# A two-layer hybrid trunk: the mixers' order on four engines laid out by a planner in the source, small transfers on SP's queue

## The chip, the cores and the metric

The kernel runs on one core of one Trainium2 chip. Its engines are TensorE (PE), VectorE (DVE), ScalarE (ACT), GpSimd (POOL) and SyncE (SP), whose queue issues most transfers. Each engine carries out its own instructions in the order in which they stand, and semaphores hold an instruction until what it needs is there. The metric is the time of one execution on the device in microseconds.

## What is computed

528 positions (16 learned meta tokens and 512 inputs) of width 1024 pass through two layers. Each layer has a mixer and a feed-forward block:

```python
def mixer_sublayer(h, ...):
    u = rms_norm(h, pre_g)
    z = jnp.einsum("bld,de->ble", u, w_in)
    q, k, v, f_logit, a_val, a_gate, sc_b, sc_c, sc_x = jnp.split(z, idx, axis=-1)
    log_f = jax.nn.log_sigmoid((f_logit + b_forget).astype(jnp.float32))
    y_attn = forgetting_attention(q.reshape(hs), k.reshape(hs), v.reshape(hs), log_f)   # 8 heads of 64
    a = a_val * jax.nn.sigmoid(a_gate)
    a = causal_depthwise_conv(a, a_dw_w) + a_dw_b                                       # 31 taps, 256 columns
    a = jax.nn.silu(layer_norm(a, a_ln_g, a_ln_b))
    y_conv = jnp.einsum("blc,ce->ble", a, a_pw_w)
    y_sc = sc_b * causal_depthwise_conv(sc_c * sc_x, sc_conv_w)                         # 3 taps, 256 columns
    y = jnp.concatenate([y_attn, y_conv, y_sc], axis=-1)
    y = jnp.einsum("ble,ed->bld", head_rms_norm(y, head_g), w_out)
    return h + rms_norm(y, post_g)

def ffn_sublayer(h, ...):
    z = causal_depthwise_conv(jnp.einsum("bld,df->blf", rms_norm(h, pre_g), w_up), conv_w)
    g, up = jnp.split(z, 2, axis=-1)
    return h + rms_norm(jnp.einsum("blf,fd->bld", jax.nn.silu(g) * up, w_down), post_g)
```

The attention's logits are q.k / 8 + F[t] - F[s] under a causal mask, with F the running sum of log_f.

## The kernel before

Everything is laid out with features on the 128 partitions and positions along the free axis, in two halves of 264 positions. Each float32 factor of a product is split into a high and a low part of a type that TensorE takes at one pass, and a product is three matmuls, high x high, low x high and high x low (`mm3`, L250). A weight chunk is 128 x 1024 (eight blocks of 128 x 128): SP loads it (`raw`, three buffers, L230), ScalarE rounds it (`whi`, L234) and VectorE subtracts (`wlo`, L235); `whi` and `wlo` have three buffers as well. A projection of one chunk is 24 matmuls of 264 columns for each half.

A mixer (`mixer`, L398) does this:

- `first` (L268): the gate and value of the conformer branch and sc_c and sc_x of the first two groups, the first half ahead of the mixer, the second half in it (L464 to L467). `gated` (L454) makes sigmoid times value out of them.
- `proj` (L411): one chunk, both halves; q, k, sc_b, sc_c, sc_x use it. `v_proj` (L610) has two chunks with the positions on the output's partitions, and 8 columns more for the forget gate (`forget_gate`, L633).
- `conv_taps` (L528): 31 taps for each of two groups, one VectorE instruction of 528 columns each; `conv_tail` (L536): layer norm, SiLU, the pointwise product and the head norms.
- `head_max` (L699): for one head, six logit matmuls (`s`), a masked maximum on VectorE (L713), its diagonal on GpSimd (L717) and one matmul that spreads it (L722). `head_exp` (L727): six blocks of keys; for each two logit matmuls (`st`, L746), exponential on ScalarE (L748), a cut on GpSimd where the block is on the diagonal (L751), rounding on ScalarE (L758), subtraction on VectorE (L759), and three matmuls with v (`acc`, L762). `att_norm` (L769): the head norm of a pair, with float32 matmuls (L777).
- `q_proj` and `k_proj` copy q and k once more by transfers (L683, L695), and `gate_rows` (L664) writes two rows of F beside each head's k (L668), for heads 4 to 7 by way of memory (`g_dram`). ScalarE's queue issues all of these.

`mixer_steps` (L110) is a list of such steps by hand, and the program is written down in its order. Which instruction stands where on an engine is then decided by the framework's scheduler, by its own estimates; only the norms' parts ahead and the output stages (`finish`, L792) have TensorE's order fixed by `manual_schedule`. PSUM has eight banks: in a mixer three `mm`, two `s1`, two `st` and one `acc` (L471 to L478, L737). After a mixer, `finish` multiplies the eight y tiles by w_out, beginning with y0, y1, y2, y4, y5, y6, then y7 and at last y3, and the feed-forward block follows.

Of the kernel before, what the change touches and what calls it, by code (L numbers as in the profile page):

```python
# [9 lines left out]
F32 = mybir.dt.float32  # L10
F32R = mybir.dt.float32r
# [25 lines left out]
NEG = -1e30  # L37

# [71 lines left out]
def mixer_steps():  # L110


    return [("sc_c", 0), ("sc_x", 0), ("sc_b", 0), ("q", 0), ("k", 0), ("v", 0), ("max", 0),
            ("q", 1), ("max", 1), ("k", 1), ("exp", 0), ("sc_norm", 0), ("max", 2), ("exp", 1), ("max", 3), ("norm", 0),
            ("v", 1), ("exp", 2), ("q", 2), ("exp", 3), ("k", 2), ("norm", 1), ("max", 4),
            ("q", 3), ("max", 5), ("exp", 4), ("k", 3), ("exp", 5), ("max", 6), ("norm", 2), ("sc_c", 1), ("max", 7),
            ("exp", 6), ("sc_x", 1), ("pw", 0), ("exp", 7), ("sc_b", 1), ("norm", 3), ("sc_norm", 1)]
# [3 lines left out]
def tile_hybrid_trunk(ctx: ExitStack, tc: tile.TileContext, xT, wflat, pv_d, out):  # L121
# [13 lines left out]
    PE = mybir.EngineType.PE  # L135
# [109 lines left out]
    def next_w():  # L245
        prefetch(1 + AHEAD)
        return ready.popleft()[1]

# [19 lines left out]
    class First:  # L268
# [3 lines left out]
        def __init__(self, rhs, n, groups):  # L272
            self.rhs, self.n, self.groups = rhs, n, groups
            self.ws, self.ps = {}, {}

        def group(self, hf, g, hooks=None):

            items = self.groups[hf][g]
            for i in items:
                if i not in self.ws:  # L280
                    self.ws[i] = next_w()
# [12 lines left out]

# [103 lines left out]
    def mixer(l, ypool, first, close_first):  # L398
# [11 lines left out]

        def proj():  # L411

            w = next_w()
            out = []
            for hf in range(2):
                d = half()[:, :H]
                mm3({hf: d}, w, range(KD), u_rhs)
                out.append((lambda t, hf=hf: t[:, half_sl(hf)], d))
            return out

        def ytiles(i):
            return (T(ypool, [P, L], F32R, f"yhi{i}"), T(ypool, [P, L], F32R, f"ylo{i}"))

        def head_norm(i, yt, hs, eps):

            yhi, ylo = ytiles(i)
            for hf in range(2):
                c = half_sl(hf)
                r = rsqrt2(mp, hs[hf], eps, H)
                nc.vector.scalar_tensor_tensor(yt[:, c], in0=yt[:, c], scalar=gcol("head_g", i), in1=r,  # L430
                                               op0=ALU.mult, op1=ALU.mult)
                nc.scalar.copy(yhi[:, c], yt[:, c])
                nc.vector.tensor_sub(ylo[:, c], yt[:, c], yhi[:, c].bitcast(F32))
            y[i] = (yhi, ylo)

        def plain_head_norm(i, yt, sq):
            hs = []
            for hf in range(2):
                nc.scalar.activation(sq[:, half_sl(hf)], yt[:, half_sl(hf)], AF.Square)
                ps = half()  # L440
                nc.tensor.matmul(ps[:, :H], lhsT=bd, rhs=sq[:, half_sl(hf)], start=True, stop=True)
                hs.append(ps[:, :H])
            head_norm(i, yt, hs, RMS_EPS)
# [3 lines left out]
        for j in range(2):  # L447
# [4 lines left out]
            conv.append(T(mp, [P, L], F32, "cacc", 2))  # L452

        def gated(hf, j):  # L454
            c = half_sl(hf)
            sig = sigs[j][:, c]
            nc.scalar.activation(sig, first.ps[hf, 2 * j], AF.Exp, scale=-1.0)
            nc.scalar.activation(sig, sig, AF.Ln, bias=c_one)
            nc.scalar.activation(sig, sig, AF.Exp, scale=-1.0)
            nc.vector.tensor_mul(apads[j][:, CK - 1 + H * hf:CK - 1 + H * (hf + 1)], first.ps[hf, 2 * j + 1], sig)  # L460

        for j in range(2):
            gated(0, j)
        for j in range(2):  # L464
            first.group(1, j)
            gated(1, j)
        first.group(1, 2)  # L467
# [3 lines left out]
        def half():  # L471
            return T(pp, [P, 512], F32, "mm", 3)

        def s1_tile():
            return T(pp, [P, 512], F32, "s1")

        def st_tile():
            return T(pp, [P, 512], F32, "st")  # L478

        ap = ms.enter_context(tc.tile_pool(name=f"ap{l}", bufs=1, side="right", reuse_waits="tile"))  # L480
# [8 lines left out]
        causal = T(ap, [P, 400], F32, "causal")  # L489
# [38 lines left out]
        def conv_taps():  # L528
            for j in range(2):
                nc.vector.tensor_scalar(conv[j], in0=apads[j][:, :L], scalar1=col("a_dw_w", CK * j),  # L530
                                        scalar2=col("a_dw_b", j), op0=ALU.mult, op1=ALU.add)
                for i in range(1, CK):
                    nc.vector.scalar_tensor_tensor(conv[j], in0=apads[j][:, i:i + L], in1=conv[j],  # L533
                                                   scalar=col("a_dw_w", CK * j + i), op0=ALU.mult, op1=ALU.add)

        def conv_tail():  # L536

            w = next_w()
            a2 = [ytiles(4), ytiles(5)]
            sq = [T(mp, [P, L + CK - 1], F32, "apad", 2) for _ in range(2)]  # L540
            for hf in range(2):
                c = half_sl(hf)
                ps = half()
                for j in range(2):
                    nc.tensor.matmul(ps[:, :H], lhsT=om_c, rhs=conv[j][:, c], start=j == 0, stop=j == 1)
                for j in range(2):
                    nc.vector.tensor_sub(conv[j][:, c], conv[j][:, c], ps[:, :H])
                    nc.scalar.activation(sq[j][:, c], conv[j][:, c], AF.Square)
                ps2 = half()
                for j in range(2):  # L550
                    nc.tensor.matmul(ps2[:, :H], lhsT=om_c, rhs=sq[j][:, c], start=j == 0, stop=j == 1)
                r = rsqrt2(mp, ps2[:, :H], LN_EPS, H)
                for j in range(2):
                    n = conv[j][:, c]
                    nc.vector.scalar_tensor_tensor(n, in0=n, scalar=gcol("a_ln_g", j), in1=r,
                                                   op0=ALU.mult, op1=ALU.mult)
                    nc.vector.tensor_scalar(n, in0=n, scalar1=col("a_ln_b", j), scalar2=None, op0=ALU.add)
                    s = sq[j][:, c]
                    nc.scalar.activation(s, n, AF.Exp, scale=-1.0)
                    nc.scalar.activation(s, s, AF.Ln, bias=c_one)  # L560
                    nc.scalar.activation(s, s, AF.Exp, scale=-1.0)
                    nc.vector.tensor_mul(n, n, s)
                    nc.scalar.copy(a2[j][0][:, c], n)
                    nc.vector.tensor_sub(a2[j][1][:, c], n, a2[j][0][:, c].bitcast(F32))
            yts = []
            for m in range(2):
                yt = T(mp, [P, L], F32, "cacc", 2)
                for hf in range(2):
                    ps = half()
                    mm3({hf: ps[:, :H]}, w, range(2), lambda b, k, hf: a2[k][b][:, half_sl(hf)],  # L570
                        cols=slice(P * m, P * (m + 1)))
                    nc.scalar.copy(yt[:, half_sl(hf)], ps[:, :H])
                yts.append(yt)
            for m in range(2):
                plain_head_norm(4 + m, yts[m], T(mp, [P, L + CK - 1], F32, "apad", 2)[:, :L])


        sc = {}

        def first_parts(i):  # L580

            return [(lambda t, hf=hf: t[:, half_sl(hf)], first.ps[hf, i]) for hf in range(2)]

        def sc_c(j):
            t = T(mp, [P, L], F32, "sccx")
            for c, ps in first_parts(4) if j == 0 else proj():
                nc.scalar.copy(c(t), ps)
            sc[j] = t

        def sc_x(j):  # L590
            t = sc[j]
# [470 lines left out]
```

## Time and profile before

| | us |
|---|---|
| median of 3 runs | 1470.01 (1466.21 to 1470.43) |
| the profiled execution | 1468.73, its span 1467.0 |
| TensorE busy, share of the span | 1326.9, 90% |
| VectorE busy, share | 906.8, 62% |
| ScalarE busy, share | 632.1, 43% |
| GpSimd busy, share | 113.4, 8% |
| mean granted TensorE clock | 0.961 |

Times in the trace count from the span's start. Mixer 0 lies between about 48 and 274 us, mixer 1 between about 778 and 1002. A row of a view by lines or of the timeline names the source line, the engine, the operation and `output<-inputs`; x is the number of instructions or matmul records (a float32 matmul shows as two), and a bracket behind it is idle time of the engine ahead of it and what ended that. A row of waits has the total, the number and the longest. The names are the tiles' tags.

### The profile page before, as it was taken

The numbers are of one execution on the slowest core, as the hardware profiler recorded it, in microseconds if no ns is written. First come the engines' busy times: TensorE is split into PE (matmuls) and PEld (weight loads), VectorE is DVE, ScalarE is ACT, GpSimd is POOL, SyncE is SP. The second block draws the span as 40 slices with busy tenths as digits, with TensorE's granted clock in tenths as the row PEclk, the third lists the DMA queues.
The fourth block names the chain that finished last, engine by engine and source line by source line (L and its number), as shares of the span: only waits on it lengthen the run. The fifth ranks groups of instructions, "written<-read, shape, count | busy, mean of one in ns | idle before, by whom it ended". The sixth has DMA issues, their size and how long they took to land.

```text
span 1467.0 us, 24898 instructions
## 1 busy us (share of the span) xinstructions
PE 1326.9 (90%) x10178; PEld 1285.5 (88%) x10178; DVE 906.8 (62%) x1616; ACT 632.1 (43%) x1189; POOL 113.4 (8%) x276
## 2 busy tenths in 40 slices
PE   4888998798999999999967989987989999999996
PEld 4888886697999999999967988866979999999995
DVE  5696655538672575467477966655477626745755
ACT  4233758635432342244342337585454323423441
POOL 1210322000000000000002103220000000000000
PEclk9999998999999999999988999988999999999998
DMA  6022110330222222323230221204202233233221
GB/s 225 15 76 86 55 55 1 131 102 29 73 87 94 94 83 91 99 89 107 87 126 16 87 75 55 55 15 146 87 15 87 87 101 97 84 94 101 83 76 58
DMA packets 42706, 118.33 MB, mean 81 GB/s; under 512 B 4848, under 2 KB 15088, under 8 KB 42592
## 3 DMA queue, kind: packets, MB, share of 16 engines
q1 hardware_dynamic: 36064, 108.77, 23.5%
q10 hardware_dynamic: 6432, 7.71, 2.0%
q8 instruction: 80, 1.31, 0.4%
q14 instruction: 34, 0.28, 0.1%
q0 software_dynamic: 96, 0.26, 0.0%
HBM read 108.04 MB, written 4.33 MB: 77 GB/s over the span
## 4 chain that ended last, share of the span: by engine, by line
PE 75%; DVE 12%; ACT 6%; DMA 5%; issue 2%; POOL 0%; ACTq 0%; DVEq 0%; POOLq 0%; SPq 0%
PE mm L256 63%; PE mm L619 4%; DMA raw<-in_w_dram 4%; DVE wlo L235 2%; DVE cacc L533 2%; PE s L256 2%; PE acc L762 2%; ACT whi L234 1%; PE st L746 1%; PE n L338 1%; DVE yp L382 1%; DVE junk L713 1%; PE s L777 1%; PE s L709 1%; ACT pf L748 1%
## 5 line engine op out<-in xcount | busy, mean ns | idle before, releaser
L256 PE MATMUL mm<-uhi,whi 128*128 128x264 f32 (+1 forms) x1888 | 441.0, 289 | 43.9 <-ACT uhi L353 16.9
L256 PE MATMUL mm<-ulo,whi 128*128 128x264 f32 (+1 forms) x1888 | 438.0, 287 | 1.2 <-DVE ulo L356 1.2
L256 PE MATMUL mm<-uhi,wlo 128*128 128x264 f32 (+1 forms) x1888 | 437.4, 287 | 0.0
L256 PEld LDWEIGHTS mm<-uhi,whi 128*128 128x128 f32 x1888 | 318.7, 192 | 48.7 <-ACT uhi L353 18.9
L234 ACT CAST whi<-raw 128x1024 fp32r<-128x1024 f32 (+3 forms) x198 | 203.0, 1030 | 327.3 <-PE mm L256 253.2
L235 DVE TENSOR_TENSOR wlo<-raw,whi 128x1024 fp32r<-128x1024 f32 (+3 forms) x198 | 236.3, 1198 | 172.1 <-ACT whi L234 165.8
L256 PEld LDWEIGHTS mm<-ulo,whi 128*128 128x128 f32 x1888 | 318.6, 192 | 2.2 <-DVE ulo L356 2.0
L256 PEld LDWEIGHTS mm<-uhi,wlo 128*128 128x128 f32 x1888 | 318.1, 192 | 0.2
L256 PE MATMUL mm<-yhi,whi 128*128 128x264 f32 (+2 forms) x976 | 228.5, 290 | 22.5 <-ACT yp L806 11.1
L256 PE MATMUL mm<-ylo,whi 128*128 128x264 f32 (+2 forms) x976 | 226.0, 287 | 1.2 <-DVE ylo L973 0.9
L256 PE MATMUL mm<-yhi,wlo 128*128 128x264 f32 (+2 forms) x976 | 225.3, 287 | 0.0
L256 PEld LDWEIGHTS mm<-yhi,whi 128*128 128x128 f32 x976 | 165.2, 193 | 26.1 <-ACT yp L806 12.5
L256 PEld LDWEIGHTS mm<-ylo,whi 128*128 128x128 f32 x976 | 165.0, 193 | 2.2 <-DVE ylo L973 1.3
L256 PEld LDWEIGHTS mm<-yhi,wlo 128*128 128x128 f32 x976 | 164.8, 192 | 0.0
L954 DVE SCALAR_TENSOR_TENSOR c<-z,pv,c 128x528 f32<-128x528 f32 (+1 forms) x176 | 132.8, 757 | 2.9
L533 DVE SCALAR_TENSOR_TENSOR cacc<-apad,pv,cacc 128x528 f32<-128x528 f32 x120 | 87.3, 763 | 0.9
L329 POOL TENSOR_TENSOR acc<-acc,c 128x528 f32<-128x528 f32 (+2 forms) x8 | 11.0, 1385 | 918.3 <-ACT c L328 918.3
L972 ACT CAST yhi<-c 128x528 fp32r<-128x528 f32 (+1 forms) x44 | 27.7, 629 | 111.1 <-DVE c L968 111.1
L937 DVE TENSOR_TENSOR z<-mm,rz 128x258 f32<-128x258 f32 (+1 forms) x88 | 33.6, 422 | 53.5 <-PE mm L256 52.9
L952 ACT ACTIVATE c<-z,pv 128x528 f32<-128x528 f32 (+1 forms) x88 | 64.1, 731 | 5.4 <-DVE z L937 5.2
L964 ACT ACTIVATE c<-c 128x528 f32<-128x528 f32 (+1 forms) x44 | 28.2, 640 | 81.0 <-DVE c L954 80.9
L934 DVE TENSOR_TENSOR z<-mm,rz 128x528 f32<-128x528 f32 x40 | 28.3, 708 | 54.6 <-PE mm L256 53.0
(193 smaller groups left out, 1647.3 us busy)
## 6 DMA issues: line engine op xcount, KB each, us to landing
raw<-in_w_dram SPq DMA_DIRECT2D x160, 512.0 KB
raw<-in_w_dram SPq DMA_DIRECT2D x32, 448.0 KB
h<-in_x_dram SPq DMA_DIRECT2D x8, 264.0 KB
h<-in_x_dram ACTq DMA_DIRECT2D x8, 264.0 KB
raw<-in_w_dram SPq DMA_DIRECT2D x4, 528.0 KB
q<-q ACTq DMA_DIRECT2D x16, 132.0 KB
k<-k ACTq DMA_DIRECT2D x16, 132.0 KB
h_dram<-h SPq DMA_DIRECT2D x4, 528.0 KB
```

What stands on the lines that cost most here:

```text
L234: nc.scalar.copy(hi[:, :sz], raw[:, :sz])
L235: nc.vector.tensor_sub(lo[:, :sz], raw[:, :sz], hi[:, :sz].bitcast(F32))
L256: nc.tensor.matmul(d, lhsT=w[a][:, k, cols], rhs=rhs(b, k, hf), start=start and i == 0 and p == 0, stop=stop and i == n - 1 and p == 2)
L533: nc.vector.scalar_tensor_tensor(conv[j], in0=apads[j][:, i:i + L], in1=conv[j], scalar=col("a_dw_w", CK * j + i), op0=ALU.mult, op1=ALU.add)
L619: nc.tensor.matmul(ps[:n, :nw], lhsT=(uhi, ulo)[ui][:, k, P * b:P * b + n], rhs=w[wi][:, k % 4, :], start=k == 0 and p == 0, stop=k == KD ...
L762: nc.tensor.matmul(acc[:, s0 - qa:qz - qa], lhsT=vt[:, b].rearrange("p h d -> p (h d)")[:, o:o + P], rhs=pt, start=b == 0 and i == 0, stop ...
L934: nc.vector.tensor_mul(two(t[:, off:]), srcs[0], two(rz))
L937: nc.vector.tensor_mul(t[:, off + a - i0:off + z - i0], src, rz[:, a:z])
L952: nc.scalar.activation(dst, src[:, 2:2 + 2 * fw], AF.Copy, scale=wtap(2, t))
L954: nc.vector.scalar_tensor_tensor(dst, in0=src[:, i:i + 2 * fw], scalar=wtap(i, t), in1=dst, op0=ALU.mult, op1=ALU.add)
L964: silu = nc.scalar.activation(cs[0], cs[0], AF.Silu)
L972: nc.scalar.copy(ghi, cs[0])
```

## The change

The mixer's steps are now short generators, threads on TensorE, that yield what they wait for. Work for ScalarE, VectorE, GpSimd and SP is not written where it stands in the source, but handed to a planner (`Flow`) with an estimated duration, the pieces of work that it waits for, and a rank. `Flow.run` goes forward in an estimated time: each engine takes, of the work that is ready, that of lowest rank number, and TensorE the first ready thread in the order maxima, head norms, exponentials, projections. Only then is the instruction written, so the program's order is the planner's; `manual_schedule` keeps it on TensorE, ScalarE, VectorE and GpSimd through the whole mixer. A thread gives TensorE back after every three matmuls of a projection. The exponentials' thread multiplies with v two blocks behind the logits (`LAG`). The taps have rank 4, weights 2, norms 1, attention and evacuations 0. `mixer_steps` now lists projections alone; v comes first, and its second half earlier. A weight chunk's load is asked for when a chunk has been used up (`plan_w`). The small transfers go to SP's queue (`dma`), whose order is still the framework's. Besides, the causal mask is bfloat16, the low part of the exponentials (`pl`) has three buffers instead of two, the taps of the two groups alternate, and the first groups keep two chunks prepared instead of three.

```diff
 def mixer_steps():
-    return [("sc_c", 0), ("sc_x", 0), ("sc_b", 0), ("q", 0), ("k", 0), ("v", 0), ("max", 0),
-            ("q", 1), ("max", 1), ("k", 1), ("exp", 0), ("sc_norm", 0), ("max", 2), ("exp", 1), ("max", 3), ("norm", 0),
...
+    return [("sc_c", 0), ("sc_x", 0), ("v", 0), ("q", 0), ("k", 0), ("sc_b", 0), ("q", 1), ("k", 1), ("v", 1),
+            ("q", 2), ("k", 2), ("sc_c", 1), ("q", 3), ("k", 3), ("pw", 0), ("sc_x", 1), ("sc_b", 1)]
+class Flow:
+    HOP = 0.06
...
+    def run(self, stop=None):
+        while True:
...
+            for eng, ops in self.pend.items():
+                can = [(r + self.HOP, o) for o in ops if (r := self.ready(o[4], o[7])) is not None]
+                if can:
+                    start = max(self.free[eng], min(r for r, _ in can))
+                    o = min((o[0], r, o[1], o) for r, o in can if r <= start)[3]
...
+            can = [(r, i) for i, t in enumerate(self.threads) if (r := self.ready(t[1])) is not None]
+            if can:
+                start = max(self.pe, min(r for r, _ in can))
...
+def mm_us(n, k=P):
+    return max(n / 2400 + 0.012, 0.00086 * k)
+def act_us(n):
+    return 0.17 + 0.0009 * n
+def dve_us(n):
+    return 0.17 + 0.00101 * n
...
+    def dma(out, in_, *after, **kw):
+        return flow.op("sp", 0.35, lambda: nc.sync.dma_start(out, in_), after, **kw)
...
+    def plan_w(freed):
...
+        got = flow.op("sp", 0.35, load, [old], lat=4.0)
+        a = act(act_us(sz), high, got, freed, prio=2)
+        box["tok"] = dve(dve_us(sz), low, a, prio=2)
...
+            for i in range(CK):
+                for j in range(2):
+                    last[j] = dve(stt_us(L), lambda j=j, i=i: tap(j, i), last[j], prio=4)
...
+        def proj(use, w=None):
+            w = yield from flow_w()
+            for hf in range(2):
+                d, slot = yield from bank("mm")
+                d = d[:, :H]
+                for k in range(KD):
+                    mm3({hf: d}, w, [k], u_rhs, start=k == 0, stop=k == KD - 1)
+                    tok = flow.mm(3 * mm_us(H))
+                    if k < KD - 1:
+                        yield
+                if hf:
+                    plan_w(tok)
+                slot.close(*use(hf, d, tok))
+                yield
...
-        causal = T(ap, [P, 400], F32, "causal")
+        causal = T(ap, [P, 400], BF16, "causal")
...
-                nc.scalar.dma_start(k2[other].bitcast(F32), k1[main].bitcast(F32))
+                q2_at[hd].append(dma(k2[other].bitcast(F32), k1[main].bitcast(F32), *k_at[hd], lat=2.2))
                 if j > 1:
-                    gate_rows(hd)
+                    gate_rows(hd, *g_done)
...
+        def exponentials():
+            blocks = [(hd, qa, qz, b) for hd in range(HEADS) for qa, qz in ((0, P), (P, L))
+                      for b in range(5) if P * b < qz]
+            boxes = []
+            for t in range(len(blocks) + LAG):
+                if t >= LAG:
...
+                    yield from weigh(*blocks[t - LAG], boxes[t - LAG])
+                    yield E_GAP
+                if t < len(blocks):
+                    hd = blocks[t][0]
+                    yield [When(lambda: max_at.get(hd)), When(lambda: q2_at.get(hd))]
+                    box = {}
+                    tok = yield from logits(*blocks[t], box)
...
-        for kind, j in mixer_steps():
-            do[kind](j)
+        for g in (maxima(), att_norms(), exponentials(), fill()):
+            flow.thread(g)
+        flow.run()
...
-                                [Group((True, 0, 1)), Group((True, 2, 3)), Group((True, 4, 5))]])
+                                [Group((True, 0, 1)), Group((True, 2, 3)), Group((True, 4, 5))]], AHEAD)
...
-        with ExitStack() as ms:
+        with ExitStack() as ms, tc.manual_schedule(engines={PE, ACT, DVE, POOL}):
             y = mixer(l, ypool, first, wxs.close)
```

What that moves is seen in the order of the instructions on each engine. First TensorE in the middle of mixer 0's attention, where one of the later heads is multiplied with v (`acc`) and the next block's or head's logits (`st`) follow. Before:

```order
L762 MATMUL acc_2334<-ph_2379,vhi_605 128x144
L746 MATMUL st_2577<-q_97_628,k_89_620 128x400
L746 MATMUL st_2577<-q_98_629,k_90_621 128x400
L762 MATMUL acc_2334<-pl_2380,vhi_605 128x144
L762 MATMUL acc_2334<-ph_2379,vlo_606 128x144
L746 MATMUL st_2589<-q_97_628,k_89_620 128x400
L746 MATMUL st_2589<-q_98_629,k_90_621 128x400
L762 MATMUL acc_2334<-p_108_658,vhi_605 128x16 x2
L762 MATMUL acc_2334<-p_108_658,vlo_606 128x16
L746 MATMUL st_2602<-q_97_628,k_89_620 128x272
```

and of the change, with a k projection (`mm`, from `uhi` and `ulo`) around it:

```order
L1161 MATMUL acc_1824<-ph_1882,vhi_621 128x144
L1161 MATMUL acc_1824<-pl_1895,vhi_621 128x144
L1161 MATMUL acc_1824<-ph_1882,vlo_622 128x144
L1100 MATMUL st_1908<-q_101_646,k_93_638 128x128
L1100 MATMUL st_1908<-q_102_647,k_94_639 128x128
L449 MATMUL mm_1860<-uhi_109,whi_1821 128x264
L449 MATMUL mm_1860<-ulo_110,whi_1821 128x264
L449 MATMUL mm_1860<-uhi_109,wlo_1837 128x264
L1161 MATMUL acc_1824<-p_109_673,vhi_621 128x16 x2
L1161 MATMUL acc_1824<-p_109_673,vlo_622 128x16
L1100 MATMUL st_1922<-q_101_646,k_93_638 128x400
L1100 MATMUL st_1922<-q_102_647,k_94_639 128x400
```

Before, no projection matmul stands in 192 such rows running, from the layer norm's first matmul to the last projection; after, projections stand between the attention steps until one head and a half are left.

Second, TensorE at the end of mixer 0: before, the last projection (sc_b, second half), the head norm of its group (`bd`), and the output product (`yhi`):

```order
L256 MATMUL mm_3049<-ulo_110,whi_2645 128x264
L256 MATMUL mm_3049<-uhi_109,wlo_2646 128x264
L441 MATMUL mm_3106<-cxp_3104,bd_88 128x264
L441 MATMUL mm_3109<-cxp_3104,bd_88 128x264
L256 MATMUL mm_3178<-yhi_271_1524,whi_2768 128x264
```

and of the change, the last head's last block, the head norm of pair 3 (`hsel`), and the output product:

```order
L1161 MATMUL acc_3029<-p_110_674,vlo_622 128x16
L1227 MATMUL s_607_3105<-sq_2811,hsel_11_92 128x264
L1227 MATMUL s_607_3105<-sq_3011,hsel_12_94 128x264
L1227 MATMUL s_610_3112<-sq_2811,hsel_11_92 128x264
L1227 MATMUL s_610_3112<-sq_3011,hsel_12_94 128x264
L449 MATMUL mm_3177<-yhi_279_1647,whi_2894 128x264
```

The short convolution's norm stood last, behind a projection; now pair 3's does, behind attention.

Third, SP's queue in mixer 0, which held weight chunks (`raw`) alone before; of the change:

```order
L417 DMA raw_1434<-in_w_dram 128x1024
L400 DMA k_87_632<-g_dram_19_114 1x528 x2
L400 DMA q_100_645<-q_99_644 64x528
L400 DMA q_102_647<-q_101_646 64x528
L417 DMA raw_1757<-in_w_dram 128x1024
L400 DMA k_92_637<-k_91_636 64x528
L400 DMA k_94_639<-k_93_638 64x528
L417 DMA raw_1764<-in_w_dram 128x1024
L400 DMA k_89_634<-g_dram_19_114 1x528 x2
L417 DMA raw_1858<-in_w_dram 128x1024
```

Gate rows of heads 4 and 5 and the copies of q and k now stand between weight chunks.

More of the change, by code (lines that the diff above doesn't have):

```diff
@@ L37 @@
 NEG = -1e30
+M_GAP = 0.0
+E_GAP = 0.0
+LAG = 2
 _COLS = {}
@@ L134, in tile_hybrid_trunk @@
     psum = [None]
-    PE = mybir.EngineType.PE
+    PE, ACT = mybir.EngineType.PE, mybir.EngineType.Activation
+    DVE, POOL = mybir.EngineType.DVE, mybir.EngineType.Pool
     def mmt():
@@ L409, in mixer @@
         y = {}
[L411 to L443, printed above, removed]
+        flow.pe = flow.now
+        for e in flow.free:
+            flow.free[e] = max(flow.free[e], flow.now)
+        zero = Tok(0.0)
         conv, apads, sigs = [], [], []
@@ new lines, in plain_head_norm @@
+        def plain_head_norm(i, yt, sq, toks, waits=()):
+            sqs = [act(act_us(H), lambda hf=hf: nc.scalar.activation(sq[:, half_sl(hf)], yt[:, half_sl(hf)], AF.Square),
+                       toks[hf], *waits) for hf in range(2)]
+            out = []
+            for hf in range(2):
+                yield [sqs[hf]]
+                ps, slot = yield from bank("mm")
+                nc.tensor.matmul(ps[:, :H], lhsT=bd, rhs=sq[:, half_sl(hf)], start=True, stop=True)
+                out.append(head_norm(i, yt, hf, ps[:, :H], slot, RMS_EPS, flow.mm(4 * mm_us(H))))
+                yield
+            return out
@@ L536, in conv_tail @@
[L536 to L575, printed above, removed]
@@ L613, in v_proj @@
             for b in range(5):
                 n = min(P, L - P * b)
-                ps = half()
+                ps, slot = yield from bank("mm")
                 for k in range(KD):
```

767 lines of the change are left out of this document (593 added, 174 removed).

## The prediction

> **What bounds the kernel now.** First the engines of the whole span and, from the slices, TensorE, VectorE and the granted clock:
>
> ```profile
> span 1467.0 us, 24898 instructions
> PE 1326.9 (90%) x10178; PEld 1285.5 (88%) x10178; DVE 906.8 (62%) x1616; ACT 632.1 (43%) x1189; POOL 113.4 (8%) x276
> PE   4888998798999999999967989987989999999996
> PEclk9999998999999999999988999988999999999998
> ```
>
> TensorE (PE) is the long engine, but its 90% is an average over two kinds of stage. The view by windows, cut where the program changes (columns: window, length, busy time and records of PE, PEld, DVE, ACT and POOL, granted clock, DMA share, GB/s):
>
> ```profile
> 48.00:203.90 155.90, 144.86 (x1092) 138.63 (x1093) 113.27 (x245) 70.47 (x173) 31.11 (x77) 0.97 0.23 64
> 203.90:261.90 58.00, 47.03 (x217) 38.15 (x216) 35.05 (x115) 42.04 (x122) 16.30 (x40) 0.82 0.06 19
> 261.90:274.40 12.50, 7.56 (x54) 6.49 (x52) 11.20 (x29) 10.13 (x27) 0.00 (x0) 0.97 0.13 43
> 380.00:520.00 140.00, 140.00 (x1152) 140.00 (x1151) 75.03 (x88) 49.48 (x64) 0.00 (x0) 1.00 0.28 91
> 778.00:933.70 155.70, 145.45 (x1095) 139.39 (x1096) 110.58 (x240) 68.98 (x171) 31.12 (x77) 0.96 0.22 64
> 933.70:989.00 55.30, 44.66 (x215) 36.04 (x215) 34.91 (x115) 42.08 (x122) 16.20 (x40) 0.88 0.07 20
> 989.00:1002.00 13.00, 7.74 (x54) 6.63 (x53) 11.33 (x30) 10.10 (x27) 0.00 (x0) 0.95 0.13 38
> ```
>
> 380 to 520 us is feed-forward: 1152 matmuls in 140 us, one every 0.1215 us, nothing lost. The two mixers are 48.0 to 274.4 and 778.0 to 1002.0. Each has a **filled** part, in which projections and attention share TensorE, then 58.0 (55.3) us of the last four heads with no projection beside them, then the last projection and its norms (12.5 and 13.0 us). These rows of the timeline and of the chain of waits set the cuts:
>
> ```profile
> 47.91 13.23 PE mm L256 x94
> 203.92 0.61 PE L545 MATMUL mm<-cacc,om_c 128*128 128x264 f32 x2
> 274.43 0.81 PE L256 MATMUL mm<-yhi,whi 128*128 128x264 f32 x2 [3.39 <-DVE rs_t L314]
> 778.02 0.59 PE L256 MATMUL mm<-uhi,whi 128*128 128x264 f32 x1 [9.17 <-DVE apad L460]
> 1002.01 0.80 PE L256 MATMUL mm<-yhi,whi 128*128 128x258 f32 x2 [3.54 <-DVE rs_t L314]
> ```
>
> A busy PE is not a PE at its pace: ends are modelled. So I count work. Two rows of the chain give prices:
>
> ```profile
> 90.29 14.59 PE mm L619 x120
> 175.56 0.89 PE s L777 x4
> ```
>
> A 264-column projection matmul costs 14.59 / 120 = 0.1216 us; a float32 one (head norms, layer norm) is two records, 2 x 0.89 / 4 = 0.445 us. Attention matmuls I price by columns, 0.1216 / 264 = 0.00046 us each (an estimate). Mixer 0 by the program's order: the filled part has 912 projection matmuls, 17 float32 ones and 34,768 attention columns: 110.9 + 7.6 + 16.0 = **134.5 us of work in 155.9 (86%)**. The unfilled part has 24 (the pointwise product), 20 and 34,736: 2.9 + 8.9 + 16.0 = **27.8 us in 58.0 (48%)**. The last has 6.7 us in 12.5. So about 57 us of this mixer's 226.4 are lost, 30 of them in the unfilled part. What TensorE waits for there, 203.9 to 261.9, longest first:
>
> ```profile
> PE s L709 <- DVE mcol L713: 1.9, 6, 0.5
> PE mm L441 <- DVE rs_t L314: 1.4, 1, 1.4
> PE mm L551 <- ACT apad L548: 1.2, 2, 0.8
> PE s L722 <- POOL dm L717: 1.0, 2, 0.7
> ```
>
> No wait is long. It is many short ones, a softmax chain through ScalarE, GpSimd and VectorE with nothing to put between, and the clock falls to 0.82 with it. ScalarE is the busiest helper (42.04 of 58.00, 72%), not saturated.
>
> **The change, part by part.** *Order on TensorE.* The number of matmuls stays; their places move. Up to the last projection matmul there now stand 960 projection matmuls (all), 25 float32 ones and 56,168 attention columns: 116.7 + 11.1 + 25.9 = **153.7 us**. Behind it stand 24 + 14 + 13,336 columns, 2.9 + 6.2 + 6.1 = **15.2 us**, one head and a half instead of four; the 48 projection matmuls that stood last are inside.
>
> The filled part's pace is what the trace can't show for the new order. Bounds: the old filled part, 86.3% (178.1 us), and feed-forward, 100% (153.7). Of the old part's 21.4 lost microseconds, 0.03 x 155.9 = 4.7 at most are clock, and the named waits are few, the two longest being
>
> ```profile
> PE mm L256 <- DVE q L678: 4.4, 4, 3.2
> PE s L648 <- DVE fpre L644: 3.1, 1, 3.1
> ```
>
> both TensorE held behind VectorE, where q's and the gate's steps stood among the convolution's taps. In the new order taps have the lowest rank and steps of three projection matmuls (0.36 us) stand between the attention steps. I take 95%, nearer to feed-forward: 161.8 us, to 47.9 + 161.8 = 209.7.
>
> The unfilled part: between TensorE's last projection and the first output matmul ScalarE has 85 instructions, in the old one 124. At 42.04 / 122 = 0.345 us each, 85 take 29.3 us if it never rests and 40.7 at the old 72%. TensorE's 15.2 us fit beneath. I take 33 us: the tail's norms are independent of the softmax chain and interleaved with it, so ScalarE should rest little. First output matmul at 242.7 instead of 274.4: **-31.7 us**. The 3.39 us wait ahead of that matmul (row above) is for the last norm to have read its PSUM bank. It stays in kind: now head pair 3's norm is last, and its wait is inside the 33.
>
> Mixer 1 starts at 778.0 as before (its 9.17 us wait is for the gating behind the pre-norm, which doesn't move) and pays 2 us for a start at half clock: 778.0 + 161.8 + 2 + 33 = 974.8 instead of 1002.0: **-27.2 us**. These rows show that start, 0.22 us from start to start, and 0.12 from 4 us on:
>
> ```profile
> 778.41 0.42 PE L256 MATMUL mm<-ulo,whi 128*128 128x264 f32 x1
> 778.63 0.42 PE L256 MATMUL mm<-uhi,wlo 128*128 128x264 f32 x1
> 782.54 0.28 PE L256 MATMUL mm<-uhi,whi 128*128 128x264 f32 x1
> 782.66 0.29 PE L256 MATMUL mm<-ulo,whi 128*128 128x264 f32 x1
> ```
>
> The Trainium skill ("TensorE: Matmul & The Clock Gate", "What's actually happening") says that an idle window of about 3.4 us halves the clock. The 9.17 us gap agrees. The 0.82 between 203.9 and 261.9 doesn't come from such gaps, since the longest named wait there is 1.4 us; that fits the same page's "A second HAM failure mode", short pauses between groups. By the first rule alone the new filled part would run at clock 1.00, up to 0.03 x 161.8 = 5 us shorter per mixer, 1400 in all.
>
> *Small transfers to SP.* These issues leave ScalarE:
>
> ```profile
> L683 ACTq DMA_DIRECT2D q<-q x16: 468/469/522, 82.5 to 919.6; - x16
> L695 ACTq DMA_DIRECT2D k<-k x16: 468/468/469, 91.7 to 921.5; - x16
> L668 ACTq DMA_DIRECT2D k<-sq x16: 538/600/1175, 129.9 to 864.1; - x16
> L668 ACTq DMA_DIRECT2D k<-g_dram x16: 209/216/394, 152.5 to 920.1; - x16
> ACT vhi L625 <- DMA k<-sq: 6.4, 1, 6.4
> ```
>
> Per mixer 8 x (0.469 + 0.468 + 0.600 + 0.216) = 14.0 us of issuing. I cost this at nothing: in the filled part ScalarE is busy 70.47 of 155.90 us, so TensorE's projections cover it, and in the tail few such issues remain. If that cover were gone, up to 14 us per mixer would be won. The Trainium skill ("DMA: Bandwidth & Descriptors", "Issuing engines are not separate DMA queues") says that the issuing engine changes only issue time; no run here shows landing times by queue, and by it the sum stays.
>
> *Weights.* A chunk is now loaded when the one three before it is done. Preparing one takes 3.19 to 4.96 us of transfer, then about 1.06 and 1.23:
>
> ```profile
> 271.72 3.19 DMA raw<-in_w_dram
> 274.93 1.06 ACT whi L234
> 276.01 1.23 DVE wlo L235
> 283.38 4.96 DMA raw<-in_w_dram
> ```
>
> 5.5 to 7.3 us, against two chunks of 48 x 0.1216 = 5.8 us, 11.7 us, of cover: hidden, 4 us to spare. The first k chunk has one chunk of cover: about 1 us, inside the 95%. *The rest* (a bfloat16 mask, a third low buffer, two chunks ahead at the first groups) moves no work between engines; nothing, bounds -1 to +1 us.
>
> **Sum:** 1468.73 (this execution; span 1467.0, and 1.3 us under the median 1470.01 of 1466.21 to 1470.43) - 31.7 - 27.2 = **1409.8 us**.
>
> **Rivals.** *Tight:* 98% and a tail of 29.3: 156.8 + 29.3 per mixer, -40.4 and -35.9: 1392. *VectorE becomes the bound:* it has 113.27 + 35.05 + 11.20 = 159.5 us per mixer, of which 65 of its instructions, at 35.05 / 115 = 0.305 us 19.8 us, are in the tail; 139.7 must pass in the filled part, 86% of 161.8 against 73% now. For it: the taps,
>
> ```profile
> L533 DVE SCALAR_TENSOR_TENSOR cacc<-apad,pv,cacc 128x528 f32<-128x528 f32 x60 | 43.5, 763 | 0.4
> 73.40:110.00 36.60, 32.79 (x256) 31.77 (x255) 36.12 (x61) 11.39 (x24) 5.89 (x17) 0.95 0.29 76
> ```
>
> 0.763 us each, stand in front of what TensorE waits for. Against: the second row, 98.7% with taps as filler. At 80% the filled part is 174.6 us: 18.9 + 14.4 won, 1435. *The order moves work, not pace:* 86.3% and 40.7 us: 266.7 and 998.8, 7.7 + 3.2 won, 1458. *Slower, through SP:* the gate rows of heads 4 to 7 can be written only when heads 0 to 3 are done, and a weight chunk stands behind each on the same queue. A head lasts 58.0 / 4 = 14.5 us; less 4 us of spare each hold could cost 10 us, 8 holds 80 us: 1490. It turns slower than before from holds of 59 / 8 + 4 = 11.4 us on. For it: SP already spends its time in waits; against: those are for raw buffers, and the gate rows stand where their head ends:
>
> ```profile
> SPq L230 <- DVE wlo L235: 1085.9, 182, 50.6
> ```
>
> *No effect:* the output stage's weights come late by what was won; 1469.
>
> **How the numbers follow.** Forecast 0.56, tight 0.10, VectorE 0.15, pace 0.10, slower through SP 0.06, no effect 0.03. Predicted 1410. The bounds of pace and tail (100% and 29.3; 90% and 40.7) give 1386 and 1443; that holds the forecast, tight and VectorE. Faster by over 0.3%, which is about what a measurement here can tell from no change: 0.56 + 0.10 + 0.15 + 0.10 = 0.91; same 0.03; slower 0.06.
>
> **What would show it.** Right: each mixer 190 to 205 us from its first half-1 group to the first output matmul; the stretch without projections 30 to 40 us; clock 0.95 or more ahead of it; waits of TensorE on VectorE under 5 us. Wrong: SP's waits for g_dram rows followed by TensorE waiting for wlo; VectorE above 95% with TensorE waiting for it; or feed-forward longer than now.

## The result, and the profile after

The changed kernel takes 1429.56 us (median of 4 runs, 1426.25 to 1432.71), the kernel before 1469.53 (4 runs beside them, 1466.21 to 1470.43). The ratio is 0.9732, with a 95% interval of 0.9705 to 0.9759: **40 us faster, where 59 were forecast**. The time lies inside the range (1386 to 1443). The profiled execution took 1428.99 us.

The page's lines on span, engines, TensorE's slices and the granted clock:

```profile
span 1427.3 us, 24874 instructions
PE 1307.3 (92%) x10178; PEld 1276.8 (89%) x10178; DVE 908.6 (64%) x1616; ACT 630.7 (44%) x1189; POOL 116.7 (8%) x268
PE   4889997798999999999967899978989999999996
PEclk9999998899999999999988999978999999999998
```

VectorE and ScalarE did the same work as before (906.8 and 632.1 us then); the span is 39.7 us shorter. The rows of TensorE's timeline that cut the stages, and in the second fence the stages themselves in the view by windows (columns as in the prediction):

```profile
47.36 0.59 PE L449 MATMUL mm<-ulo,whi 128*128 128x264 f32 x1 [0.17 <-DVE ulo L554]
215.96 0.28 PE L449 MATMUL mm<-uhi,wlo 128*128 128x264 f32 x1
250.60 0.75 PE L449 MATMUL mm<-yhi,whi 128*128 128x264 f32 x1
755.60 0.59 PE L449 MATMUL mm<-uhi,whi 128*128 128x264 f32 x1 [9.16 <-DVE apad L630]
958.73 0.79 PE L449 MATMUL mm<-yhi,whi 128*128 128x258 f32 x1
```

```profile
47.40:216.10 168.70, 163.44 (x1250) 158.71 (x1251) 134.32 (x327) 90.97 (x234) 45.24 (x103) 0.97 0.21 60
216.10:250.60 34.50, 25.50 (x113) 20.25 (x112) 25.04 (x58) 29.55 (x85) 3.79 (x10) 0.81 0.12 38
755.60:923.90 168.30, 162.13 (x1251) 157.19 (x1252) 130.71 (x321) 89.71 (x232) 44.96 (x103) 0.99 0.21 60
923.90:958.70 34.80, 26.09 (x113) 21.03 (x112) 25.12 (x58) 29.60 (x85) 3.63 (x10) 0.79 0.13 37
958.70:1008.70 50.00, 42.76 (x311) 41.63 (x310) 15.56 (x20) 18.01 (x27) 2.56 (x2) 0.87 0.45 145
```

In mixer 0 the filled part now holds one more projection and two and a half more heads, and it grew from 156 to 168.7 us; what stands behind it fell from 70.5 to 34.5. The 19.2 us that are missing against the sum of 1409.8 stand in these places:

| | forecast | measured | missing |
|---|---|---|---|
| mixer 0: filled part | 161.8 | 168.7, begun 0.5 early | 6.4 |
| mixer 0: tail | 33 | 34.5 | 1.5 |
| first output matmul to mixer 1 | 503.6 | 505.0 | 1.4 |
| mixer 1: filled part (with 2 us for the start) | 163.8 | 168.3 | 4.5 |
| mixer 1: tail | 33 | 34.8 | 1.8 |
| first output matmul to the end | 465.0 | 468.6 | 3.6 |

What TensorE waits for in mixer 0's filled part, longest first (total, times, longest), is little (a wait of 4.0 us for the pre-norm stands ahead of it, as before the change):

```profile
PE mm L449 <- DVE wlo L425: 1.8, 1, 1.8
PE mm L895 <- DVE vlo L881: 1.7, 1, 1.7
PE s L1080 <- POOL dm L1071: 1.4, 2, 0.7
```

The 1.8 us are the stall at the first k chunk that the prediction named. These waits are 4.9 us, and the clock of 0.97 is 0.03 x 168.7 = 5 us at most. Half of that is the mixer's start: up to 53.2 us, 25 projection matmuls follow each other in 0.22 us instead of 0.12, some 2.5 us. The forecast had a term for such a start in mixer 1 alone. Most of the rest of the 15.0 us between 153.7 and 168.7 is work that I priced too low. These rows of mixer 0's timeline show it, where TensorE has no idle time:

```profile
144.04 0.28 PE L895 MATMUL mm<-wlo,uhi 128*128 128x256 f32 x1
144.16 0.28 PE L1080 MATMUL s<-dm,ones_r 128*128 128x264 f32 x1
...
146.24 0.22 PE L1161 MATMUL acc<-ph,vhi 128*128 128x128 f32 x1
146.30 0.27 PE L1161 MATMUL acc<-pl,vhi 128*128 128x128 f32 x1
146.41 0.28 PE L1161 MATMUL acc<-ph,vlo 128*128 128x128 f32 x1
146.52 0.57 PE L1100 MATMUL st<-q,k 128*128 128x400 f32 x2
...
213.64 0.26 PE L1161 MATMUL acc<-p,vlo 128*128 128x16 f32 x1
213.75 0.37 PE L1056 MATMUL s<-k,q 128*128 128x272 f32 x1
```

From start to start a matmul of 256 columns takes 0.12 us, one of 128 columns 0.11, and one of 16 columns 0.11 as well. By columns the last two would take 0.059 and 0.007. Only the first of a group of three, right behind a wide matmul, is shorter (0.06 at 146.24). Between 130 and 216 us the median is 0.111 us for the weighing's matmuls of 128, of 144 and of 16 columns, and 0.182 for 400, which is by columns. The filled part has 88 such narrow matmuls (up to 144 columns) with 128 weight columns. Their times from start to start add up to 9.0 us in either mixer; by columns they would be 4.5, so this is **4.5 us more per mixer** than in my 153.7. Waits, clock and this floor come to 14.4 of mixer 0's 15.0 us. In mixer 1 they are 5.8, at most 1.7 (clock 0.99) and 4.5, of 14.6; 2.6 us stay unexplained there. The Trainium skill ("TensorE: Matmul & The Clock Gate", "LDWEIGHTS (loading the stationary operand)") says that loading weights takes as many cycles of 1.2 GHz as there are weight columns; by that I estimate 107 ns for 128 and 13 ns for 16. The trace agrees for 128 (0.111 us). Matmuls of 16 columns with only 16 weight columns follow each other in 0.027 us between 130 and 216 us: far shorter, but twice the estimate.

### The profile page after: what moved, and what is told of

It reads as the page before. It is cut to its first block, busy times and chain, and to the rows that moved or that the text cites. A ratio compares the mean times of both kernels' runs of the same rounds, so it can differ in the third digit from the quotient of the medians.

```text
span 1427.3 us, 24874 instructions
## 1 busy us (share of the span) xinstructions
PE 1307.3 (92%) x10178; PEld 1276.8 (89%) x10178; DVE 908.6 (64%) x1616; ACT 630.7 (44%) x1189; POOL 116.7 (8%) x268
## 4 chain that ended last, share of the span: by engine, by line
PE 81%; DVE 6%; ACT 5%; DMA 4%; POOL 2%; issue 2%; DVEq 0%; ACTq 0%; POOLq 0%
PE mm L449 68%; DMA raw<-in_w_dram 4%; PE mm L895 3%; PE acc L1161 3%; PE s L449 2%; PE st L1100 1%; ACT whi L373 1%; DVE wlo L374 1%; PE s L1227 1%; PE n L536 1%; PE s L1056 1%; DVE yp L580 1%; POOL q L294 1%; DVE acc L527 1%; POOL k L294 1%
## 5 line engine op out<-in xcount | busy, mean ns | idle before, releaser
L449 PE MATMUL mm<-uhi,whi 128*128 128x264 f32 (+1 forms) x1888 | 441.7, 289 | 34.5 <-ACT uhi L551 17.4
L373 ACT CAST whi<-raw 128x1024 fp32r<-128x1024 f32 (+2 forms) x162 | 165.8, 1028 | 282.7 <-PE mm L449 226.2
L374 DVE TENSOR_TENSOR wlo<-raw,whi 128x1024 fp32r<-128x1024 f32 (+2 forms) x162 | 193.4, 1198 | 131.5 <-ACT whi L373 125.2
```

Source lines behind the costliest of these rows:

```text
L373: nc.scalar.copy(hi[:, :sz], raw[:, :sz])
L374: nc.vector.tensor_sub(lo[:, :sz], raw[:, :sz], hi[:, :sz].bitcast(F32))
L449: nc.tensor.matmul(d, lhsT=w[a][:, k, cols], rhs=rhs(b, k, hf), start=start and i == 0 and p == 0, stop=stop and i == n - 1 and p == 2)
```

## The experiments

All ratios are to the kernel before, run beside them, and the changed kernel's is 0.9732. "Mixer" means the time from the first matmul of the half-1 groups to the first output matmul, and "filled part" that up to the last projection matmul: 204.0 and 203.1 us, and 169.4 and 168.2, in the changed kernel (mixer 0 begins at 46.6 here, one matmul earlier than in the rows above).

### E1 and E2: the small transfers

```diff
-        return flow.op("sp", 0.35, lambda: nc.sync.dma_start(out, in_), after, **kw)
+        return flow.op("sp", 0.35, lambda: nc.scalar.dma_start(out, in_), after, **kw)
```

> The changed kernel with its small transfers (q, k, gate rows) issued by ScalarE again; every other instruction stays where it is on its engine. My theory (the move to SP is worth nothing, because ScalarE is busy 89.7 of the 168.3 us of mixer 1's filled part): 1429.6 +- 4 us, mixers 203 +- 2 us. Rival (the issues stood on the path): up to 14.0 us more per mixer, 1458, most of it in the filled part.

1433.27 us, ratio 0.9772 (0.9736 to 0.9807); mixers 203.2 and 204.5. In the kernel before, the opposite edit:

```diff
-                nc.scalar.dma_start(q2[main].bitcast(F32), q1[main].bitcast(F32))
+                nc.sync.dma_start(q2[main].bitcast(F32), q1[main].bitcast(F32))
...
```

> The kernel before with only the four kinds of small transfers moved from ScalarE's queue to SP's. My theory (nothing): 1469.5 +- 4. Rival (ScalarE's 14.0 us of issuing per mixer stood on the path): down to 1441. The rival on the other side (the transfers hold SP's queue, and the weights behind them): above 1474, with TensorE waiting for wlo.

1466.08 us, ratio 0.9978 (0.9958 to 0.9998). Both say 3 to 6 us for the whole kernel, and neither says much more than nothing: the changed kernel's interval and E1's overlap, and E2's ends at 0.2 thousandths from no change. The 28 us of the rival are excluded. Two rows of SP's own waits in the changed kernel show what stands in its queue, and three of its timeline what that does to the weights in mixer 0:

```profile
SPq L400 <- ACT q L982: 70.7, 6, 33.0
...
SPq L400 <- ACT k L1010: 21.5, 4, 5.6
```

```profile
59.59 0.33 SPq L417 DMA_DIRECT2D raw<-in_w_dram  x1
91.50 1.16 SPq L400 DMA_DIRECT2D q<-q  x2
92.75 1.25 SPq L417 DMA_DIRECT2D raw<-in_w_dram  x2
```

A small transfer holds SP's queue for up to 33.0 us, and the weights issued behind it wait too. TensorE's wait for `wlo` is 1.8 us in mixer 0's filled part all the same, and it is 1.8 us in E1 too, where these transfers are not in SP's queue: so it doesn't come from there.

### E3: VectorE relieved

```diff
-                nc.vector.scalar_tensor_tensor(conv[j], in0=src, in1=conv[j], scalar=col("a_dw_w", CK * j + i),
+                nc.vector.scalar_tensor_tensor(conv[j][:, :64], in0=src[:, :64], in1=conv[j][:, :64], scalar=col("a_dw_w", CK * j + i),
```

> The changed kernel with 60 of the convolution's 62 taps per mixer cut from 528 columns to 64 (the convolution's result is left incomplete); every instruction stays in its place. VectorE loses about 60 x (0.763 - 0.285) = 28.7 us of its 131 us in each filled part. My theory (VectorE doesn't set the pace there; TensorE waits for it 3.5 us in 168.7): 1429.6 +- 5, mixers 203 +- 2.5. Rival (VectorE bound, whose forecast of 1435 lies nearest to the result): filled parts 10 us or more shorter each, 1409 or less.

1419.54 us, ratio 0.9677 (0.9646 to 0.9707); mixers 198.9 and 198.2. The group of the taps in mixer 0, and the two windows of that mixer:

```profile
L639 DVE SCALAR_TENSOR_TENSOR cacc<-apad,pv,cacc 128x64 f32<-128x64 f32 x60 | 14.9, 276 | 0.1
```

```profile
46.40:212.30 165.90, 162.49 (x1250) 157.82 (x1251) 107.98 (x329) 91.64 (x234) 41.20 (x103) 0.98 0.21 61
212.30:245.30 33.00, 22.94 (x114) 17.80 (x113) 24.86 (x57) 29.15 (x84) 4.00 (x10) 0.93 0.11 34
```

Neither forecast held. VectorE's busy time in the filled part fell from 134.3 to 108.0 us, and the part became 3.5 us shorter (3.3 in mixer 1), the tail 1.6. TensorE's waits for `wlo`, 1.8 and 1.9 us in the changed kernel, are gone from the two filled parts. So VectorE delays TensorE a little, but it is no bound: an eighth of its saving arrives. The VectorE rival's 1435 was the forecast nearest to the result, and its mechanism is not what happened.

### E4: only TensorE's order fixed

```diff
-        with ExitStack() as ms, tc.manual_schedule(engines={PE, ACT, DVE, POOL}):
+        with ExitStack() as ms, tc.manual_schedule(engines={PE}):
```

> The changed kernel with only TensorE's order fixed in the mixers; VectorE, ScalarE and GpSimd are ordered by the framework's scheduler, as before the change. My theory (the gain is TensorE's order, projections beside the heads): 1430 to 1445. Rival (the helpers' fixed order carries it): 1455 or more.

1451.99 us, ratio 0.9889 (0.9860 to 0.9919), between the two forecasts; mixers 217.1 and 216.5. The loss stands in the filled parts, 186.6 and 186.9 us; the tails are even 4 to 5 us shorter. The longest waits of TensorE on VectorE in mixer 0's filled part, and a piece of VectorE's timeline there:

```profile
PE s L928 <- DVE fpre L923: 6.3, 1, 6.3
...
PE s L927 <- DVE fe L920: 3.4, 1, 3.4
PE acc L1161 <- DVE pl L1133: 2.8, 2, 1.7
```

```profile
96.84 1.45 DVE L639 SCALAR_TENSOR_TENSOR cacc<-apad,pv,cacc 128x528 f32<-128x528 f32 x2
98.21 0.16 DVE L923 TENSOR_TENSOR fpre<-fpre,fe 128x8 f32<-128x8 f32 x1
98.29 1.44 DVE L639 SCALAR_TENSOR_TENSOR cacc<-apad,pv,cacc 128x528 f32<-128x528 f32 x2
99.64 0.16 DVE L923 TENSOR_TENSOR fpre<-fpre,fe 128x8 f32<-128x8 f32 x1
99.72 1.44 DVE L639 SCALAR_TENSOR_TENSOR cacc<-apad,pv,cacc 128x528 f32<-128x528 f32 x2
```

The scheduler puts two taps, 1.44 us, between any two sums of the forget gate, which take 0.16 us each and on which the first head waits. That is the 3.1 us wait for `fpre` of the kernel before, again. **The fixed order on the three helpers together is worth 22 us on top of TensorE's, over half of the gain**; TensorE's order with the helpers free brings 16 (by the ratio).

### E5: narrow matmuls twice

```diff
+                twice = qz - s0 < 200
+                for again in range(1 + twice):
-                nc.tensor.matmul(acc[:, s0 - qa:qz - qa],
+                    nc.tensor.matmul(acc[:, s0 - qa:qz - qa],
...
```

> The changed kernel in which each of the weighing's narrow matmuls (128, 144 and 16 columns, 72 per mixer) is done twice (so the weights of those blocks count double in the output); every order stays. Floor theory (a matmul with 128 weight columns takes 0.111 us from start to start however narrow it is): some 58 of the 72 lie in the filled part, 58 x 0.111 = 6.4 us per mixer, 12.9 in all: 1442 +- 3. By columns, as I priced them: 58 x 0.044 = 2.6 per mixer: 1434.5. If TensorE had room there: 1429.6.

1444.65 us, ratio 0.9824 (0.9795 to 0.9854): 13.5 us more by the ratios and 15.1 by the medians for 144 more matmuls, about 0.1 each. By columns it would have been 144 x 0.044 = 6.3 us. The filled parts are 174.0 and 175.1 us (54 of the 72 lie there, not 58): 4.6 and 7.0 more, together 11.6 against 2 x 54 x 0.111 = 12.0. From start to start the narrow matmuls of a filled part now add up to 15.0 us instead of 9.0, 0.111 for each added one. So the floor is real and stands on the path.

### E6 and E9: the tail's clock

```diff
+            ps, slot = yield from bank("mm")
+            while HEADS // 2 - 1 not in norm_mm:
+                nc.tensor.matmul(ps[:, :H], lhsT=uhi[:, 0, :P], rhs=uhi[:, 0, :H], start=True, stop=True)
+                tok = flow.mm(mm_us(H))
+                yield
+            slot.close(tok)
```

> The changed kernel with one more thread behind the last projection: matmuls of 264 columns into a bank that nobody reads, at the lowest rank, until the last head's norm is on TensorE. Theory (the clock halves in the tail, 6.5 and 7.3 us of full-speed time lost there, and makes the fixed orders misfit): tails 34.5 and 34.8 us fall to about 30, ScalarE's busy time there being 29.6; with the output stage's start at full clock 1414 to 1422. Rival (ScalarE's chain sets the tail whatever the clock, and the added matmuls and the bank they hold stand in the way): 1430 to 1437, as the planner's own end is 3.5 us later per mixer.

1446.65 us, ratio 0.9827 (0.9790 to 0.9864): 14 us slower than the changed kernel by the ratios, and outside both forecasts. The tails are 31.5 us and the clock in them 1.00, but the bank that the thread holds is missing for the norms of the convolution's product. They slid behind the first output matmul, as two waits around the start of the output stage show:

```profile
PE mm L449 <- DVE rs_t L779: 3.7, 1, 3.7
PE mm L807 <- DVE rs_t L779: 2.1, 1, 2.1
```

So E6 changes two things. E9 puts the same matmuls into a bank that stands free (`bank("s1")`, from the last maxima to the last weighing):

> The same idea as in the run with the warm tail, with another bank: the matmuls that nobody reads go into a bank of the row maxima, which stands free from the last head's maxima to its last weighing, so that no norm waits for a bank. The planner's own end is 0.55 us later per mixer than the changed kernel's. Theory (the half clock in the tail costs time, there and at the output stage's start): tails 34.5 and 34.8 us fall to 30 to 32, no half clock before the output stage, its first part as before the change; 1416 to 1424. Rival (ScalarE's chain sets the tail at any clock): 1428 to 1433.

1426.49 us, ratio 0.9702 (0.9670 to 0.9735); mixers 202.8 and 204.0. The two tails:

```profile
215.90:250.50 34.60, 32.52 (x234) 30.40 (x232) 24.88 (x59) 29.83 (x83) 5.08 (x10) 1.00 0.15 46
926.80:961.30 34.50, 32.42 (x232) 30.32 (x231) 24.85 (x59) 29.74 (x83) 5.10 (x10) 1.00 0.16 47
```

Clock 1.00 instead of 0.81 and 0.79, ScalarE as busy as before, and the tails as long as before: **the half clock there costs nothing that shows**. That is the rival, though the time lies between the two forecasts. What the added matmuls themselves cost in the tail isn't measured; the planner counted 0.55 us per mixer. The 3 to 4 us against the changed kernel are within the two intervals, so E9 is not shown to be better.

### E7 and E8: what the planner's rules are worth

E7 takes out the `yield` within a bank of a projection; E8 gives the taps `prio=0` instead of 4.

> The changed kernel with a projection laid out in steps of one bank (24 matmuls, 2.9 us) instead of 3 matmuls (0.36 us). Theory (the fine steps are half of the gain, since an attention step that is ready waits for the step before it to end): the planner's own end is 25.5 us later per mixer, so 1480. Rival (only the order of whole projections and heads matters): 1430 to 1442.

> The changed kernel with the convolution's taps ranked with attention's steps (0) instead of last (4); the planner lays everything out anew. Theory (VectorE has time enough but only if taps fill its pauses; a tap of 0.763 us ahead of a softmax step delays TensorE): the planner's own end is 28.5 us later per mixer, so about 1485. Rival (VectorE has slack, its order doesn't matter): 1430 to 1440.

E7: 1483.61 us, ratio 1.0081 (1.0049 to 1.0113); E8: 1474.88, ratio 1.0028 (1.0010 to 1.0046). **Each one undoes the whole gain.** E7's windows in mixer 0, then E8's longest waits of TensorE in mixer 0's filled part:

```profile
46.20:223.70 177.50, 166.86 (x1192) 159.14 (x1193) 131.10 (x300) 84.57 (x211) 37.04 (x87) 0.91 0.20 60
223.70:281.70 58.00, 40.23 (x172) 32.77 (x171) 31.43 (x88) 39.12 (x109) 9.27 (x26) 0.68 0.06 19
```

```profile
PE mm L449 <- DVE wlo L425: 13.5, 1, 13.5
PE s L928 <- DVE fpre L923: 6.4, 1, 6.4
```

With steps of 2.9 us a head that is ready waits for the end of a step, so fewer heads get done beside projections (172 matmul records in the tail instead of 113), and the tail is 58.0 us again. With taps at attention's rank, weight chunks and gate sums queue behind taps. The planner's own count of a mixer was near in both: 228.3 against 235.5 and 231.6 us measured in E7, 231.3 against 229.2 and 229.6 in E8, and 202.8 against 204.0 and 203.1 in the changed kernel.

### E10 and E11: another plan

```diff
-            nc.scalar.copy(box["hi"][:, :sz], box["raw"][:, :sz])
+            nc.gpsimd.tensor_copy(box["hi"][:, :sz], box["raw"][:, :sz])
-            g = act(act_us(H), lambda: nc.scalar.copy(yhi[:, c], yt[:, c]), f)
+            g = pool(0.75, lambda: nc.gpsimd.tensor_copy(yhi[:, c], yt[:, c]), f)
...
```

> The changed kernel with two kinds of copies (rounding a weight chunk, rounding a norm's output) moved from ScalarE to GpSimd, the pointwise product and one query projection placed earlier, and two ranks changed; this is the best of some 900 plans by the planner's own count, which ends 5.2 us earlier per mixer (197.5 instead of 202.8; GpSimd's copies are set at 1.43 and 0.75 us). Theory (ScalarE's work sets the tail, 29.6 us busy of 34.5): 1417 to 1424. Rival (GpSimd's copies take longer than set, or slow VectorE): 1430 to 1450.

> The two preceding edits together. Theory (clock and ScalarE's work are separate costs): both gains, 1405 to 1416. Rival (either one takes the other's gain): no better than the better of the two.

E10: 1435.98 us, ratio 0.9771 (0.9745 to 0.9797). E11: 1431.48, ratio 0.9739 (0.9714 to 0.9765). E10's windows in mixer 0:

```profile
45.90:229.80 183.90, 173.99 (x1271) 167.06 (x1272) 148.94 (x345) 83.47 (x233) 65.80 (x128) 0.94 0.20 58
229.80:254.40 24.60, 19.13 (x94) 15.08 (x92) 19.26 (x42) 18.47 (x53) 9.28 (x17) 0.86 0.12 43
```

The tail is 10 us shorter, the filled part 14 us longer, and the mixer takes 208.3 us where the planner counted 197.5. GpSimd's copies are not the reason by themselves: a chunk took 1.065 us, less than the 1.43 set. The taps took 0.793 us instead of 0.764, and TensorE waited 3.6 us for `fpre`. The clock was 0.94 instead of 0.97, 0.03 x 183.9 = 5.5 us at most, and the filled part holds more of attention. What else the plan missed wasn't found. E11 mixes the plan with E9's thread; it isn't faster than the changed kernel.

### E12: no weights prepared in the tail

```diff
+        if chunks[i][0] == "w_out":
+            return
         wpos[0] += 1
```

> The changed kernel in which the planner no longer prepares the output projection's weight chunks (three per mixer: 3 x 1.05 us of ScalarE and 3 x 1.22 us of VectorE in the tail of 34.5 us); the output stage prepares them. The order ahead of the tail stays. Theory (the softmax chain sets the tail, ScalarE's load only in part, as the planner counts it: its end is 1.8 us earlier per mixer): tails 32.5 to 33. Rival (ScalarE's load sets it: 29.6 - 3.15): tails 31.4 or less. Rival (neither): 34.5. In all cases the output stage pays for a late first chunk, 4 to 7 us per mixer by one chunk's transfer and roundings, so 1430 to 1440 in all.

1429.36 us, ratio 0.9715 (0.9685 to 0.9746), as the changed kernel. It settles nothing on the tail, since the edit doesn't do what it should: the output stage's roundings were put into the tail all the same, as a row of ScalarE's timeline shows,

```profile
252.57 1.04 ACT L373 CAST whi<-raw 128x1024 fp32r<-128x1024 f32 x1
```

and ScalarE has 85 instructions there as before. The tails took 37.7 and 37.8 us, at clocks of 0.74 and 0.78, in a profiled execution of 1436.33 us, the longest of the four; why they are longer stays open.

## Why the prediction was right, and where it was off

- *The mechanism: projections beside heads, one head and a half left for the tail.* Right. All four signs came: mixers of 204.0 and 203.1 us (190 to 205 forecast), stretches without projections of 34.5 and 34.8 (30 to 40), clock 0.97 and 0.99 ahead of them, and 3.7 us of waits on VectorE in mixer 0's filled part (under 5).
- *The pace of the filled part, 95% of 153.7 us.* This is the step that failed in size. It took 168.7 and 168.3 us. The 95% was near; the work under it was too little: "Attention matmuls I price by columns" leaves out 4.5 us per mixer, as the start-to-start rows show and E5 confirms. With 158.2 us of work the pace is 94%. The old filled part is short of the floor as well; the error grows with the change because more heads move into the part that TensorE bounds (88 narrow matmuls instead of 58).
- *The helpers' order.* The prediction named the two waits that go, 7.5 us, and the taps' last rank, and hid what they are worth in the 95%. E4 and E8 show that it is the greater part: 22 us are lost with the scheduler's order on the three helpers, 45 with taps in front. No run frees VectorE's order alone. The forecast of the total doesn't suffer from it; the weight that it gives to its reasons does.
- *The tail, 33 us.* 34.5 and 34.8. ScalarE had 85 instructions and 29.6 us of work, as forecast (29.3). A clock held at 1.00 doesn't shorten it (E9). In E10 ScalarE had 53 instructions and 18.5 us of work in a tail of 24.6. That the 5 to 6 us above its work are the softmax chain's waits between its instructions fits these rows, but no run took them away alone: this stays open.
- *Small transfers at nothing.* 3 us in E2, with an interval that nearly reaches zero. A term of nothing was near enough.
- *Weights hidden.* Right but for 1.8 us at the first k chunk, where about 1 was named. With the taps shortened (E3) this wait is gone: VectorE's load makes it, not the chunk's transfer, which was issued by 59.59 us.
- *The rest (mask, third low buffer, two chunks ahead) at nothing.* No run took these out. The masked maxima take VectorE 0.428 us with the bfloat16 mask and 0.422 before (medians of 80), so the mask brings nothing there.
- *The rest of the kernel unchanged.* 5.0 us were given back there, all in the output stages. The sign of error that the prediction named, a longer feed-forward, did not come: from layer 0's first feed-forward matmul to mixer 1 it takes 412.6 us (412.5 before), and from layer 1's to the end 374.7 (374.8). Of the 5.0, 1.1 and 1.0 are a wait for the last norm that now stands behind the first output matmul instead of ahead of it:

```profile
252.44 0.39 PE L449 MATMUL mm<-yhi,whi 128*128 128x264 f32 x1 [1.08 <-DVE rs_t L779]
960.56 0.58 PE L449 MATMUL mm<-yhi,whi 128*128 128x256 f32 x1 [1.04 <-DVE rs_t L779]
```

  After mixer 1 the clock in the first 50 us was 0.87 (0.91 in the kernel before), about 2 us. In E9, where the clock was full up to the output stage, the two stretches came to 506.8 and 465.3 us instead of 505.0 and 468.6, so no steady gain hangs on it.
- *The rivals.* Of the VectorE bound, E3 leaves 5 us per mixer. SP's queue did fill with waits and hurt nobody. "Order moves work, not pace" is refuted: with the floor counted in both, TensorE's pace in the filled part went from an estimated 88% (some 3 us for the 58 narrow matmuls on top of 134.5, in 155.9) to 94%.

## What to carry to other kernels

Price matmuls by their start-to-start times in the trace, shape by shape: narrow ones with full weights have a floor, and it counts just where TensorE becomes the bound. Where an order is laid out by hand, bulk work on a helper (here the taps) belongs at the last rank, and the filler on TensorE in short steps (0.36 us here; with 2.9 the gain was gone, and nothing between was run). Either rule broken cost the whole gain. A result that lies nearest to a rival's time doesn't prove the rival: relieve the suspected engine with every instruction left in its place, and look.

## What the runs showed of the hardware that was not expected

In a run of narrow matmuls with 128 weight columns, each behind the first takes 0.111 us from start to start at 16 columns as at 144, while one of 16 columns with 16 weight columns takes 0.027. And TensorE's granted clock stood at 0.8 for 34 us at no cost that could be measured, where TensorE was not what the stretch waited for: with the clock held at 1.00 by matmuls that nobody reads, those stretches took 34.6 and 34.5 us instead of 34.5 and 34.8.
